# A two-layer hybrid SSM/retention/GLA backbone: opening chunks re-queued, modulation loads halved, norms rounded straight from PSUM, and layer 1's pack copies read from SBUF

## Chip, cores and metric

The kernel runs on one core of one Trainium2 chip. The metric is device time in microseconds for one execution; the time before is 1385.05 us, the median of three runs (1379.94, 1385.05, 1386.57).

## What is computed

Two layers of a diffusion backbone work on 256 latent tokens `x` and 256 context tokens `ctx`, D = 1024, all in fp32. Cut to what matters:

```
for l in range(2):
    m_l = split((silu(c)     @ w_mod[l] + b_mod[l]), 6)      # modulation vectors, latent
    m_c = split((silu(c_ctx) @ w_mod[l] + b_mod[l]), 6)      # modulation vectors, context
    p_l = split_in(modulate(rms_norm(x,   norm_mix[l]), m_l[0], m_l[1]) @ w_in[l])
    p_c = split_in(modulate(rms_norm(ctx, norm_mix[l]), m_c[0], m_c[1]) @ w_in[l])
    s5, ret, gla = three parallel token mixers on the columns of p_c, p_l
    x = x + m_l[2] * (merge(s5, ret, gla, gates) @ w_out[l])
    x = x + m_l[5] * swiglu(modulate(rms_norm(x, norm_ffn[l]), m_l[3], m_l[4]))
    # ctx gets the same two updates in layer 0 only
return rms_norm(x, norm_final)
```

`modulate(h, shift, scale)` is `h * (1 + scale) + shift`. Before anything of layer 0 can be projected, its first two modulation vectors (shift and scale, 2 x 1024 columns of `w_mod`, 8 MB) have to be computed.

## The kernel before

**Precision.** Every fp32 matmul is made of three matmuls in fp32r: an operand is split into a rounded part `hi` and a remainder `lo`, and `hi*hi + hi*lo + lo*hi` is summed. For weights, ACT writes `hi <- raw` (L228) and DVE writes `lo <- raw - hi` (L231); for activations the pair lives in `rb` (tile block, hi or lo, k, 128 tokens). Weights come through a ring of three `raw` buffers and four `hi`/`lo` pairs, loaded ahead of use by a scheduler's priorities.

**Who orders the work.** Code is traced with priorities, and a scheduler that simulates the engines decides the order in which each engine's instructions stand. At run time every engine takes its own list strictly from the front. `tc.issue_after(ins)` adds an order only: what is traced inside it on that engine stands behind `ins`. All loads named here (`in_w_mod`, `in_w_in`) are issued by SP in one list.

**The opening of layer 0** (`layer`, l == 0). The first D of the modulation is cut into four chunks c of 256 columns for shift and scale each. For each chunk: `mod_chunk` loads `w_mod` (two loads of 1 MB, one for each of m = 1 and 0), runs 8 + 64 small matmuls against `sil` (`b<-wm,one`, `b<-arena,sil` or `b<-zone,sil`), copies the result to SBUF on ACT (`arena<-b 128x128`), transposes it on PE and writes `mod` on DVE. `norm_chunk` transposes the chunk's 256 channels of all four token tiles into two PSUM banks (s = 0 context, 1 latent), modulates them on DVE (`arena<-b,mod`, multiply then add), rounds them on ACT (`rb<-arena`) and takes the remainder on DVE (`rb<-arena,rb`). `pack_weights` loads and splits the chunk's 512 KB of `w_in`, and `pack_mms` runs 24 matmuls of 128x128 by 128x512 into four banks that all four chunks add into. When chunk 3 is done, `pack_out` copies the four banks out (`arena<-b 128x512` on ACT, `perm` on DVE, L593), and `gla_v` starts: its weights are four loads of 416 KB, `raw 128x832`.

**Two places in layer 1.** `pack_early` and `pack` also end in `pack_out`, there with `lean=True`: ACT copies each bank to `res[x]`, and DVE reads the same bank again for the permuted copy `up` that is stored to DRAM. After the output projection, `out_tok` calls `norm_t` for tile 3 and then tile 2, and `ffn_in_tok` begins with `p == 0`: 24 matmuls for each tile. `norm_t` transposes a tile in two halves of four k; of each half ACT modulates two k and DVE two into `h32`, ACT rounds `h32` into `rb`, DVE takes the remainder.

Of the kernel before, what the change touches and what calls it, by code (L numbers as in the profile page):

```python
# [19 lines left out]
D = 1024  # L20
KD = 8
# [118 lines left out]
class Hybrid:  # L140
# [86 lines left out]
    def act(self, out, in_, f, scale=1.0, bias=0.0):  # L227
        self.S.activation(out, in_, f, bias=bias, scale=scale)  # L228
# [202 lines left out]
    def mod_chunk(self, c, brow):  # L431
# [3 lines left out]
        for m in (1, 0):  # L435
            ws[m] = (self.zone if c == 3 and m else self.arena).new(KD, 256)
            self.q["modc"].dma_start(out=ws[m].ap, in_=i["w_mod"][0][:, D * m + 256 * c:D * m + 256 * c + 256].rearrange(
                "(k p) c -> p k c", p=128))
# [12 lines left out]
        self.act(rows.ap, b[:, :128], AF.Copy)  # L451
        tb = self.bank()
# [8 lines left out]
    def norm_chunk(self, c, xs):  # L461
        ks = slice(2 * c, 2 * c + 2)
        h32 = self.new(4, 2, 128)
        for s in range(2):
            b = self.bank()
            for t in range(2):
                for k in range(2):
                    o = 128 * (2 * t + k)
                    self.transpose(b[:, o:o + 128], xs[2 * s + t].ap[:, 128 * (2 * c + k):128 * (2 * c + k) + 128])
            hv = h32.ap[:, 2 * s:2 * s + 2]  # L470
            bc = lambda a: a[:, None, ks, s:s + 1].to_broadcast([128, 2, 2, 128])
# [51 lines left out]
    def norm_t(self, l, which, t, x):  # L523
# [66 lines left out]
    def pack_out(self, pk, banks, u_dr, res=None, lean=False):  # L590
# [4 lines left out]
        for x in range(4):  # L595
# [3 lines left out]
            perm(up.ap[:, c0:], banks[x][:, c0:])  # L599
# [4 lines left out]
            if lean and x == 0:  # L604
                perm(up.ap[0:64, 0:256], banks[0][0:64, 0:256])
# [824 lines left out]
    def ffn_in_tok(self, l):  # L1430
# [3 lines left out]
        for p in range(KF // 2):  # L1434
# [10 lines left out]
            if not p:  # L1445
                self.tok_mms(banks, ws, (1, 0), range(KD), 0, KD - 1, h)
# [52 lines left out]
    def layer(self, l):  # L1499
# [5 lines left out]
        if l == 0:  # L1505
            with self.prio(-2 * W_AHEAD):
# [8 lines left out]
                banks = [self.bank(self.mm) for _ in range(4)]  # L1515
                for c in range(4):
# [3 lines left out]
                self.drop(*xs)  # L1520
            gqk = self.pack_out(0, banks, u_dr)
            self.load_params2()
# [8 lines left out]
        if l == 0:  # L1531
            self.s5d = [{}, {}]
            self.gd = [{m: self.dram.tile([2, D], F32, name=self.nm("gd")) for m in (2, 5)} for _ in range(2)]
            with self.inside(self.zone):
                self.s5_tables()
# [110 lines left out]
```

## Time and profile before

| | |
|---|---|
| Median of three runs | 1385.05 us |
| The profiled execution's own time | 1389.15 us |
| Its span, first to last instruction | 1387.1 us |
| PE busy | 1332.2 us, 96% of the span |
| DVE / ACT busy | 909.6 us (66%) / 579.1 us (42%) |
| Mean granted TensorE clock | 0.986 of 2.4 GHz |
| HBM read / written | 231.0 MB / 23.3 MB |

The profiled execution is 4.1 us longer than the median of the runs, and all sums below are made against it. In rows of the timeline the first number is the start in us, the second the length, then engine, line, operation, what it writes and reads, the count, and in brackets the idle time before it and what ended it. A clock of 1.00 is 2.4 GHz, 0.50 is 1.2 GHz.

### The profile page before, as it was taken

To read this page: it belongs to the slowest core of one execution; us is meant where nothing else is said; L and a number is where in the kernel's file an instruction comes from. 1 tells how busy PE (TensorE), PEld (TensorE's weight loads), DVE (VectorE), ACT (ScalarE), POOL (GpSimd) and SP (SyncE) were. 2 spreads that over 40 slices of the span, in tenths; PEclk is the share of its full clock that TensorE was granted. 3 is DMA by queue.
4 is the path that set the end of the run, shared out by engine and by line. 5 is a ranking of instruction groups with operands and counts; after the bars stand their busy time and mean duration, and the time that the engine had idled before them with its cause. 6 is when DMAs were issued, how large, how long until landed. Compare 5 with 4: busy or idle time off the path is not lost.

```text
span 1387.1 us, 20296 instructions
## 1 busy us (share of the span) xinstructions
PE 1332.2 (96%) x7723; PEld 1082.7 (78%) x7723; DVE 909.6 (66%) x1395; ACT 579.1 (42%) x920; POOL 73.7 (5%) x115
## 2 busy tenths in 40 slices
PE   4899999999999999999999999999999989899997
PEld 3788888777767778788777777898987867788886
DVE  4579682849879665535455687764696688655555
ACT  3367352333432233222222345544456544544453
POOL 3310000002000020000000000000000010000000
PEclk9999999999999999999999999999999989999999
DMA  9743455677877565633333787654655646465653
GB/s 308 205 123 106 153 167 165 228 220 236 280 245 216 200 184 170 215 92 106 119 115 116 250 310 245 197 158 122 181 160 189 199 145 213 149 194 187 213 183 106
DMA packets 202584, 255.63 MB, mean 184 GB/s; under 512 B 20704, under 2 KB 153100, under 8 KB 201976
## 3 DMA queue, kind: packets, MB, share of 16 engines
q1 hardware_dynamic: 189032, 228.05, 52.6%
q10 hardware_dynamic: 10240, 20.39, 4.1%
q0 software_dynamic: 3216, 5.91, 1.7%
q8 instruction: 61, 1.00, 0.3%
q14 instruction: 35, 0.29, 0.1%
HBM read 231.00 MB, written 23.30 MB: 183 GB/s over the span
## 4 chain that ended last, share of the span: by engine, by line
PE 81%; DMA 8%; DVE 5%; issue 2%; ACT 2%; SPq 1%; POOL 0%; DVEq 0%; ACTq 0%; POOLq 0%
PE b L243 79%; DMA wm<-in_w_mod_dram 4%; PE b L253 2%; DVE arena L231 1%; DVE zone L234 1%; DVE lo L231 1%; DMA arena<-in_w_mod_dram 1%; DMA raw<-in_w_in_dram 1%; ACT arena L228 1%; DMA arena<-udr 1%; ACT hi L228 1%; DMA arena<-sw 1%; DMA arena<-in_ctx_dram 0%; DMA raw<-in_w_ffn_out_dram 0%; DMA rb<-k 0%
## 5 line engine op out<-in xcount | busy, mean ns | idle before, releaser
L243 PE MATMUL b<-hi,rb 128*128 128x512 f32 (+2 forms) x1752 | 535.5, 383 | 5.5 <-DVE arena L593 3.5
L243 PE MATMUL b<-rb,hi 128*128 128x512 f32 (+1 forms) x1568 | 465.3, 378 | 1.4 <-DVE rb L231 1.4
L231 DVE TENSOR_TENSOR lo<-raw,hi 128x1024 fp32r<-128x1024 f32 (+3 forms) x295 | 333.7, 1136 | 201.4 <-ACT hi L228 198.5
L228 ACT ACTIVATE hi<-raw 128x1024 fp32r<-128x1024 f32 (+3 forms) x295 | 289.7, 989 | 419.4 <-PE b L243 275.0
L243 PEld LDWEIGHTS b<-hi,rb 128*128 128x128 f32 x1752 | 328.1, 189 | 67.4 <-issue 8.1
L243 PE MATMUL b<-lo,rb 128*128 128x512 f32 (+2 forms) x876 | 334.2, 382 | 0.9 <-DVE lo L231 0.9
L243 PEld LDWEIGHTS b<-rb,hi 128*128 128x128 f32 x1568 | 284.5, 189 | 64.5 <-issue 11.9
L243 PE MATMUL b<-rb,lo 128*128 128x512 f32 (+1 forms) x784 | 294.2, 376 | 0.0
L243 PEld LDWEIGHTS b<-lo,rb 128*128 128x128 f32 x876 | 166.2, 190 | 28.3 <-issue 1.6
L243 PEld LDWEIGHTS b<-rb,lo 128*128 128x128 f32 x784 | 147.9, 189 | 28.6 <-issue 3.4
L228 ACT ACTIVATE arena<-b 128x512 f32<-128x512 f32 (+7 forms) x168 | 79.1, 481 | 106.1 <-PE b L243 71.8
L243 PE MATMUL b<-arena 128*128 128x96 f32 (+9 forms) x1056 | 120.7, 289 | 0.8 <-ACT arena L228 0.8
L231 DVE TENSOR_TENSOR arena<-arena 128x512 f32<-128x512 f32 (+5 forms) x164 | 102.0, 640 | 17.2 <-ACT arena L228 14.9
L243 PEld LDWEIGHTS b<-arena 128*128 128x128 f32 (+6 forms) x1056 | 89.9, 160 | 24.3 <-issue 8.3
L234 DVE SCALAR_TENSOR_TENSOR arena<-arena,b 128x512 f32<-128x512 f32 (+1 forms) x124 | 72.3, 587 | 47.4 <-PE b L243 44.3
L234 DVE SCALAR_TENSOR_TENSOR zone<-wm,sil,zone 128x1024 f32<-128x1024 f32 x56 | 71.0, 1280 | 26.1 <-DMA wm<-in_w_mod_dram 26.0
L231 DVE TENSOR_TENSOR zone<-zone 128x512 f32<-128x512 f32 (+3 forms) x117 | 67.9, 604 | 28.5 <-DMA wb<-zone 17.4
L228 ACT ACTIVATE rb<-arena 128x256 fp32r<-128x256 f32 (+3 forms) x101 | 46.4, 476 | 61.5 <-PE b L243 33.6
L231 DVE TENSOR_TENSOR rb<-arena,rb 128x256 fp32r<-128x256 f32 (+2 forms) x106 | 53.7, 521 | 16.9 <-ACT rb L228 16.7
L253 PE MATMUL b<-cst,arena 128*128 128x128 f32 (+2 forms) x254 | 40.0, 284 | 19.4 <-DMA arena<-in_norm_mix_dram 8.9
L253 PEld LDWEIGHTS b<-cst,arena 128*128 128x128 f32 (+2 forms) x254 | 30.9, 146 | 27.3 <-issue 16.1
L228 ACT ACTIVATE arena<-arena 128x512 f32<-128x512 f32 (+3 forms) x62 | 36.7, 599 | 34.9 <-DVE arena L231 27.8
(145 smaller groups left out, 686.5 us busy)
## 6 DMA issues: line engine op xcount, KB each, us to landing
wm<-in_w_mod_dram SPq DMA_DIRECT2D x80, 512.0 KB
raw<-in_w_ffn_out_dram SPq DMA_DIRECT2D x66, 512.0 KB
raw<-in_w_in_dram SPq DMA_DIRECT2D x48, 512.0 KB
raw<-in_w_ffn_in_dram SPq DMA_DIRECT2D x44, 512.0 KB
raw<-in_w_ffn_in_dram SPq DMA_DIRECT2D x88, 256.0 KB
raw<-in_w_in_dram SPq DMA_DIRECT2D x48, 384.0 KB
raw<-in_w_out_dram SPq DMA_DIRECT2D x16, 512.0 KB
arena<-in_w_mod_dram SPq DMA_DIRECT2D x7, 1024.0 KB
```

Source lines behind the costliest of these rows:

```text
L228: self.S.activation(out, in_, f, bias=bias, scale=scale)
L231: self.last = self.V.tensor_tensor(out=out, in0=a, in1=b, op=op).ins
L234: self.last = self.V.scalar_tensor_tensor(out=out, in0=a, scalar=s, in1=b, op0=op0, op1=op1).ins
L243: self.last_mm = self.P.matmul(out, l, r, start=start, stop=stop, **k).ins
L253: self.last_tr = self.P.transpose(out, in_, self.ident[:k, :k]).ins
```

## The change

1. `mod_chunk` loads each chunk of `w_mod` as four loads of 512 KB, the first four k of both m ahead of the last four.
2. `norm_chunk` no longer goes through an SBUF copy to be rounded: for each k of each bank ACT writes the modulated and rounded value from PSUM into `rb`, DVE writes the unrounded one from the same PSUM columns into `h32`, and DVE takes the remainder per bank.
3. The opening's `pack_mms` of chunk c is traced behind the norm of chunk c + 1, and the ACT part of `pack_weights` stands behind the ACT copy of the chunk's modulation (`row_out`).
4. `load_params2` and `s5_tables` stand behind the opening's last matmul on PE, `s5_tables` also behind the last norm instruction on ACT.
5. `norm_t` is written as `norm_chunk` is now, four k on each engine.
6. With `lean`, `perm` reads ACT's SBUF copy, not the bank; ACT copies the context half of bank 0's first 64 partitions too.
7. `ffn_in_tok`, `p == 0`: for each tile first all `hi` by `hi` and `hi` by `lo` matmuls, then those with the tile's `lo`.

```diff
         for m in (1, 0):
             ws[m] = (self.zone if c == 3 and m else self.arena).new(KD, 256)
-            self.q["modc"].dma_start(out=ws[m].ap, in_=i["w_mod"][0][:, D * m + 256 * c:D * m + 256 * c + 256].rearrange(
-                "(k p) c -> p k c", p=128))
+        for kh in range(2):
+            for m in (1, 0):
+                self.q["modc"].dma_start(out=ws[m].ap[:, 4 * kh:4 * kh + 4], in_=i["w_mod"][0][
+                    512 * kh:512 * kh + 512, D * m + 256 * c:D * m + 256 * c + 256].rearrange("(k p) c -> p k c", p=128))
...
-            self.tt(hv, b.rearrange("p (t k c) -> p t k c", t=2, k=2), bc(self.mod[:, 0, 1]), ALU.mult)
-            self.tt(hv, hv, bc(self.mod[:, 0, 0]), ALU.add)
-        self.act(self.rb[:, 1:5, 0, ks], h32.ap, AF.Copy)
-        self.tt(self.rb[:, 1:5, 1, ks], h32.ap, self.rb[:, 1:5, 0, ks].bitcast(F32), ALU.subtract)
-        self.drop(h32)
+            for k in range(2):
+                kk = 2 * c + k
+                src = b[:, 256 * k:256 * k + 256].rearrange("p (t c) -> p t c", t=2)
+                self.act(self.rb[:, rows, 0, kk], src, AF.Identity, scale=sc[:, kk, s:s + 1], bias=sh[:, kk, s:s + 1])
+                self.ts(h32.ap[:, :, k], src, sc[:, kk, s:s + 1], sh[:, kk, s:s + 1], ALU.mult, ALU.add)
+            self.tt(self.rb[:, rows, 1, ks], h32.ap, self.rb[:, rows, 0, ks].bitcast(F32), ALU.subtract)
...
-                src, dst = b[:, 128 * k:128 * k + 128], h32.ap[:, kk]
-                if k < 2:
-                    self.act(dst, src, AF.Identity, scale=sc[:, kk, s:s + 1], bias=sh[:, kk, s:s + 1])
-                else:
-                    self.ts(dst, src, sc[:, kk, s:s + 1], sh[:, kk, s:s + 1], ALU.mult, ALU.add)
-            self.act(self.rb[:, 1 + t, 0, ks], h32.ap[:, ks], AF.Copy)
+                src = b[:, 128 * k:128 * k + 128]
+                self.act(self.rb[:, 1 + t, 0, kk], src, AF.Identity, scale=sc[:, kk, s:s + 1], bias=sh[:, kk, s:s + 1])
+                self.ts(h32.ap[:, kk], src, sc[:, kk, s:s + 1], sh[:, kk, s:s + 1], ALU.mult, ALU.add)
...
-            perm(up.ap[:, c0:], banks[x][:, c0:])
+            if lean and x == 0:
+                self.act(o.ap[0:64, 0:256], banks[0][0:64, 0:256], AF.Copy)
+            perm(up.ap[:, c0:], (o.ap if lean else banks[x])[:, c0:])
...
                 for c in range(4):
                     self.mod_chunk(c, brow)
                     self.norm_chunk(c, xs)
-                    self.pack_mms(banks, self.pack_weights(0, 0, c), c)
+                    with self.tc.issue_after(self.row_out):
+                        ws.append(self.pack_weights(0, 0, c))
+                    if c:
+                        self.pack_mms(banks, ws[c - 1], c - 1)
+                self.pack_mms(banks, ws[3], 3)
```

On ACT, where the opening's last two chunks stood before (`hi_501` is chunk 3's weights, `b_343` and `b_437` are the modulation of chunks 2 and 3, `hi_639` to `hi_726` are the first three weights of `gla_v`):

```order
L228 ACTIVATE hi_407<-raw_404 128x16x16
L228 ACTIVATE hi_501<-raw_498 128x16x48
L228 ACTIVATE hi_501<-raw_498 128x16x16
L228 ACTIVATE arena<-b_343 128x128
L228 ACTIVATE hi_639<-raw_636 128x832
L228 ACTIVATE hi_683<-raw_680 128x832
L228 ACTIVATE arena<-b_437 128x128
L228 ACTIVATE rb<-arena 128x4x256 x2
L228 ACTIVATE zone<-zone 128x32
L228 ACTIVATE hi_726<-raw_723 128x832
```

The same place on ACT in the changed kernel (`b_431` is chunk 3's modulation, `hi_501` its weights, `b_478` and `b_488` its two banks of transposed tokens, `hi_663` to `hi_750` the first three weights of `gla_v`):

```order
L228 ACTIVATE arena<-b_431 128x128
L228 ACTIVATE hi_501<-raw_498 128x16x48
L228 ACTIVATE hi_501<-raw_498 128x16x16
L228 ACTIVATE hi_663<-raw_660 128x832
L228 ACTIVATE hi_707<-raw_704 128x832
L228 ACTIVATE rb<-b_478,mod 128x2x128
L228 ACTIVATE rb<-b_488,mod 128x2x128
L228 ACTIVATE hi_750<-raw_747 128x832
L228 ACTIVATE rb<-b_478,mod 128x2x128
L228 ACTIVATE rb<-b_488,mod 128x2x128
```

The copy of a chunk's modulation now stands ahead of the weights, and one weight of `gla_v`, `hi_750`, stands between the first and second k of chunk 3's norm, where the before had its third weight behind the whole norm. DVE's list has the same shape: `lo_708` stands ahead of chunk 3's `mod`, and `lo_751` between the first and the second k. On SP the third weight's load, `raw_747`, now stands behind two loads of 512 KB of later modulation weights (`wm`); before, the third weight stood ahead of those two.

On PE, at the start of layer 1's FFN: before (`b_9656`, `b_9667` are tile 3's transposes, `b_9711`, `b_9722` tile 2's, `b_9734` and `b_9733` the sums of tiles 3 and 2):

```order
L253 MATMUL b_9656<-cst,arena 128x128 x4
L253 MATMUL b_9667<-cst,arena 128x128 x4
L253 MATMUL b_9711<-cst,arena 128x128 x4
L253 MATMUL b_9722<-cst,arena 128x128 x4
L243 MATMUL b_9734<-hi_9738,rb 128x512
L243 MATMUL b_9734<-lo_9739,rb 128x512
```

And in the changed kernel, with `b_9682`, `b_9696` for tile 3, `b_9743`, `b_9757` for tile 2, `b_9772`, `b_9771` the sums:

```order
L253 MATMUL b_9682<-cst,arena 128x128 x4
L253 MATMUL b_9696<-cst,arena 128x128 x4
L243 MATMUL b_9772<-hi_9776,rb 128x512
L243 MATMUL b_9772<-lo_9777,rb 128x512
L243 MATMUL b_9772<-hi_9776,rb 128x512
L243 MATMUL b_9772<-lo_9777,rb 128x512
L253 MATMUL b_9743<-cst,arena 128x128 x4
L243 MATMUL b_9772<-hi_9783,rb 128x512
L243 MATMUL b_9772<-lo_9784,rb 128x512
L243 MATMUL b_9771<-hi_9776,rb 128x512
```

Four FFN matmuls of tile 3 now stand between tile 3's and tile 2's transposes. Elsewhere the scheduler's lists differ in many small places; the largest on PE is in layer 0's gates, where the third of the groups `b<-zone,unit` that close a modulation vector summed on DVE stands 72 matmuls of 512 columns earlier than before.

## Rows read from the trace of the kernel before

**Rows 1.** The page: busy time, share of the span and instructions of each engine.
```profile
PE 1332.2 (96%) x7723; PEld 1082.7 (78%) x7723; DVE 909.6 (66%) x1395; ACT 579.1 (42%) x920; POOL 73.7 (5%) x115
```

**Rows 2.** Windows (us; busy PE, PEld, DVE, ACT, POOL; PEclk, DMA share, GB/s).
```profile
30.00:40.00 10.00, 9.98 (x78) 7.37 (x77) 4.09 (x7) 2.21 (x3) 6.07 (x12) 1.00 1.10 339
40.00:50.00 10.00, 7.53 (x102) 5.86 (x104) 5.07 (x12) 3.10 (x5) 3.47 (x7) 0.72 0.87 256
44.40:51.20 6.80, 6.30 (x81) 4.94 (x81) 6.03 (x12) 2.24 (x4) 2.57 (x6) 0.50 0.73 220
1187.90:1194.70 6.80, 4.69 (x15) 4.08 (x16) 6.16 (x12) 4.02 (x10) 0.56 (x1) 0.50 0.06 9
400.00:420.00 20.00, 17.00 (x84) 12.09 (x83) 16.50 (x20) 7.51 (x12) 0.00 (x0) 0.91 0.76 230
```

**Rows 3.** Timeline of SP's queue in the opening.
```profile
12.43 3.67 SPq L437 DMA_DIRECT2D arena<-in_w_mod_dram  x2
...
36.28 10.34 SPq L273 DMA_DIRECT2D raw<-in_w_in_dram  x6
47.69 0.82 SPq L357 DMA_DIRECT2D wm<-in_w_mod_dram  x2
```

**Rows 4.** Timeline of the opening's end, chunks 2 and 3.
```profile
41.35 1.07 PE L243 MATMUL b<-arena,sil 128*32 128x128 f32 x30
...
43.54 1.15 ACT L228 ACTIVATE hi<-raw 128x768 fp32r<-128x768 f32 x2 [7.21 <-DMA raw<-in_w_in_dram]
...
44.90 0.48 PE L253 MATMUL b<-cst,arena 128*128 128x128 f32 x1 [2.47 <-ACT arena L228]
...
46.51 0.90 ACT L228 ACTIVATE hi<-raw 128x832 fp32r<-128x832 f32 x1 [0.27 <-DMA raw<-in_w_in_dram]
...
47.73 1.02 DVE L231 TENSOR_TENSOR lo<-raw,hi 128x832 fp32r<-128x832 f32 x1
...
59.55 1.30 PE L243 MATMUL b<-rb,hi 128*128 128x512 f32 x5
...
65.00 0.35 PE L243 MATMUL b<-hi,rb 128*128 128x416 f32 x1
```

**Rows 5.** Timeline of chunk 0's norm: multiply, round, remainder.
```profile
22.20 1.29 DVE L231 TENSOR_TENSOR arena<-b,mod 128x512 f32<-128x512 f32 x2
...
24.72 1.06 ACT L228 ACTIVATE rb<-arena 128x1024 fp32r<-128x1024 f32 x1 [3.38 <-DVE arena L231]
...
25.81 1.23 DVE L231 TENSOR_TENSOR rb<-arena,rb 128x1024 fp32r<-128x1024 f32 x1 [1.12 <-ACT rb L228]
```

**Rows 6.** Timeline of layer 1's first norm, rounded from PSUM already.
```profile
915.64 2.84 ACT L228 ACTIVATE rb<-b,mod 128x256 fp32r<-128x256 f32 x6 [4.42 <-PE b L253]
916.24 2.37 DVE L240 TENSOR_SCALAR arena<-b,mod 128x256 f32<-128x256 f32 x5 [2.13 <-ACT rb L228]
...
919.57 0.68 DVE L231 TENSOR_TENSOR rb<-arena,rb 128x512 fp32r<-128x512 f32 x1
```

**Rows 7.** Timeline where layer 1's FFN begins.
```profile
1186.54 1.06 PE L253 MATMUL b<-cst,arena 128*128 128x128 f32 x8 [1.79 <-DVE arena L238]
...
1187.65 1.48 ACT L228 ACTIVATE arena<-b,mod 128x128 f32<-128x128 f32 x4
...
1190.01 1.94 PE L253 MATMUL b<-cst,arena 128*128 128x128 f32 x8 [2.41 <-DVE arena L238]
...
1191.61 0.78 PE L243 MATMUL b<-hi,rb 128*128 128x512 f32 x1
...
1192.61 1.05 PE L243 MATMUL b<-hi,rb 128*128 128x512 f32 x2
```

**Rows 8.** Timeline behind layer 1's second pack.
```profile
970.50 0.37 ACT L228 ACTIVATE arena<-b 128x256 f32<-128x256 f32 x1
...
971.18 0.74 DVE L593 COPY arena<-b 128x256 f32<-128x256 f32 x2
...
972.06 0.41 PE L243 MATMUL b<-hi,rb 128*128 128x384 f32 x1 [1.70 <-DVE arena L593]
```

More of the change, by code (lines that the diff above doesn't have):

```diff
@@ L227, in act @@
     def act(self, out, in_, f, scale=1.0, bias=0.0):
-        self.S.activation(out, in_, f, bias=bias, scale=scale)
+        self.last_act = self.S.activation(out, in_, f, bias=bias, scale=scale).ins
     def tt(self, out, a, b, op):
@@ L451, in mod_chunk @@
         self.act(rows.ap, b[:, :128], AF.Copy)
+        self.row_out = self.last_act
         tb = self.bank()
@@ L462, in norm_chunk @@
         ks = slice(2 * c, 2 * c + 2)
-        h32 = self.new(4, 2, 128)
+        sh, sc = self.mod[:, 0, 0], self.mod[:, 0, 1]
         for s in range(2):
             b = self.bank()
-            for t in range(2):
-                for k in range(2):
-                    o = 128 * (2 * t + k)
-                    self.transpose(b[:, o:o + 128], xs[2 * s + t].ap[:, 128 * (2 * c + k):128 * (2 * c + k) + 128])
-            hv = h32.ap[:, 2 * s:2 * s + 2]
-            bc = lambda a: a[:, None, ks, s:s + 1].to_broadcast([128, 2, 2, 128])
-            self.tt(hv, b.rearrange("p (t k c) -> p t k c", t=2, k=2), bc(self.mod[:, 0, 1]), ALU.mult)
-            self.tt(hv, hv, bc(self.mod[:, 0, 0]), ALU.add)
-        self.act(self.rb[:, 1:5, 0, ks], h32.ap, AF.Copy)
-        self.tt(self.rb[:, 1:5, 1, ks], h32.ap, self.rb[:, 1:5, 0, ks].bitcast(F32), ALU.subtract)
-        self.drop(h32)
+            h32 = self.new(2, 2, 128)
+            rows = slice(1 + 2 * s, 3 + 2 * s)
+            for k in range(2):
+                for t in range(2):
+                    o = 128 * (2 * k + t)
+                    self.transpose(b[:, o:o + 128], xs[2 * s + t].ap[:, 128 * (2 * c + k):128 * (2 * c + k) + 128])
+            for k in range(2):
+                kk = 2 * c + k
[3 more added lines that the diff above has]
+            self.tt(self.rb[:, rows, 1, ks], h32.ap, self.rb[:, rows, 0, ks].bitcast(F32), ALU.subtract)
+            self.drop(h32)
+        self.norm_act = self.last_act
     def gate_rows(self, gd):
@@ L604, in pack_out @@
             if lean and x == 0:
-                perm(up.ap[0:64, 0:256], banks[0][0:64, 0:256])
+                perm(up.ap[0:64, 0:256], o.ap[0:64, 0:256])
                 self.q["up"].dma_start(out=u_dr[128 * pk:128 * pk + 64, :, 0:32],
@@ L1445, in ffn_in_tok @@
             if not p:
-                self.tok_mms(banks, ws, (1, 0), range(KD), 0, KD - 1, h)
+                for t in (1, 0):
+                    for k in range(KD):
+                        for x in range(2):
+                            self.mm_(banks[t], h(t, k)[0], ws[k // 2][x][:, k % 2], k == 0 and x == 0, False)
+                    for k in range(KD):
+                        self.mm_(banks[t], h(t, k)[1], ws[k // 2][0][:, k % 2], False, k == KD - 1)
             gt = [self.new(256) for _ in range(2)]
@@ L1515, in layer @@
                 banks = [self.bank(self.mm) for _ in range(4)]
+                ws = []
                 for c in range(4):
@@ L1518, in layer @@
                     self.norm_chunk(c, xs)
-                    self.pack_mms(banks, self.pack_weights(0, 0, c), c)
+                    with self.tc.issue_after(self.row_out):
[3 more added lines that the diff above has]
+                self.pack_mms(banks, ws[3], 3)
                 self.drop(*xs)
+            pe, act = self.last_mm, self.norm_act
             gqk = self.pack_out(0, banks, u_dr)
-            self.load_params2()
+            with self.tc.issue_after(pe):
+                self.load_params2()
         else:
@@ L1533, in layer @@
             self.gd = [{m: self.dram.tile([2, D], F32, name=self.nm("gd")) for m in (2, 5)} for _ in range(2)]
-            with self.inside(self.zone):
+            with self.inside(self.zone), self.tc.issue_after(pe), self.tc.issue_after(act):
                 self.s5_tables()
```

## The prediction

> **What bounds the kernel now.** I read the page first: PE is busy 96% of the span, DVE 66% [rows 1]. A change can therefore win only where PE stands idle, runs at half clock, or has matmuls taken away, and none are taken away here. So I went through the waits of PE and the windows with a low granted clock, and then through the timeline of the three places where the change meets such a wait. The reader should see three things.
>
> First, the opening is bound by its loads: 339 GB/s from 30 to 40 us [rows 2], chunk 3's weights landed at 43.54, where ACT began to split them [rows 4]. That split stood in ACT's list ahead of chunk 2's modulation copy, although chunk 2's modulation matmuls had ended at 42.42; PE idled 2.47 us until 44.90 [rows 4], and from 44.4 to 51.2 its granted clock was 0.50, 1.2 GHz [rows 2]. Everything behind followed: pack of chunk 3 at 59.55, first `gla_v` matmul (`128x416`) at 65.00 [rows 4]. Second, at the start of layer 1's FFN two idle times of 1.79 and 2.41 us end at 1186.54 and 1190.01 [rows 7], and the clock is 1.2 GHz from 1187.9 to 1194.7 [rows 2]. Third, behind layer 1's second pack PE waits 1.70 us for DVE's copies [rows 8].
>
> PE has hardly a gap behind the opening, so I let what is saved there pass whole to the end. That is an assumption, and rival 2 takes it away.
>
> **Opening, term A.** Chunk 3's modulation weights stand ahead of 512 KB of its `w_in`, so they land about 512 KB / 339 GB/s = 1.5 us before 43.54, at 42.0. PE has then only the later half of their matmuls to do (the whole 72 take some 1.07/30 each): with the split loads the first half is done; 0.5 us more for the end gives 42.5. The 20 matmuls left of chunk 2's pack at (65.00 − 59.55)/24 = 0.227 us [rows 4] make 4.5 us: 47.0. Nine transposes (eight took 1.06 [rows 7]) end at 48.1, and the eight matmuls of the two packs left that need no remainder (1.8) at 49.9. From there PE needs the norm of chunk 3.
>
> That norm's `mod` stands behind `lo` of `gla_v`'s second weight on DVE: its `hi` began at 46.51 and took 0.90, the `lo` 1.02 [rows 4], so 48.4, and `mod` is there at about 48.8. Then the new queue decides. ACT has the third weight's `hi_750` between the first and second k. Its load stands on SP behind chunk 3's weights, two weights of 416 KB and two loads of 512 KB: with its own 416 KB that is 2272 KB after 43.54, 6.9 us at 339 GB/s or 9.1 us at the 256 GB/s of 40 to 50 us [rows 2], so 50.4 to 52.6; I take 51.5. Then `hi` 0.90, two Identities from PSUM at 2.84/6 = 0.47 each, the last multiply-add on DVE at 2.37/5 = 0.47 (both [rows 6]) give 53.8; DVE's own `lo_751` (1.02) lies beside the Identities. Two remainders of 0.68 [rows 6]: 55.2. Twenty matmuls of chunk 3 follow, 4.55 us: 59.7. PE will have been idle about 5 us before them, twice what came ahead of the half clock at 44.90, so part of them will run at 1.2 GHz. A stretch of 6.8 us at half clock [rows 2] loses 3.4 us; bounds are 0 and 3.4, and I take the middle, 1.7, since the eight matmuls before the wait and the 20 behind it are fewer than those of the old stretch. `gla_v` begins at 61.4 to 61.5: **A = 3.5 us**. Bounds: with the third weight at 52.6 and the whole 3.4 the start is 64.3, gain 0.7. If the weight is never late, the norm goes from 48.8 through five steps of 0.47 (ACT and DVE by turns on two banks) and two remainders to 52.5, the matmuls end at 57.1, gain 7.9.
>
> The new norm itself is no longer than the old one. Before, a bank took multiply and add (0.65 each), and a rounding of 1.06 and a remainder of 1.23 for both banks [rows 5]; from 22.20 to 27.04, 4.8 us. Now 5 × 0.47 + 1.36 = 3.7 us for both. By turns is how the row behaves: the first multiply-add at 916.24 waited for ACT's `rb` [rows 6].
>
> The Trainium skill, "PSUM — Partial Sum Buffer", section "PSUM bank collisions raise a hardware error", asks for just that: two engines must not touch one bank in the same partitions at once, reads against reads included. It speaks against the change, which gives ACT and DVE the same bank to read four times in turn; the trace agrees in its wait at 916.24. If the two could read side by side, the chain above would be two steps, about 0.9 us, shorter.
>
> **Layer 1's FFN, term B.** Four matmuls of tile 3 now stand ahead of tile 2's transposes. Before, PE idled 2.41 us there [rows 7]; they need only `hi` of tile 3's first k. At half clock two take 1.05, so four take some 2.0 us [rows 7], which fills the idle time before 1190.01 nearly whole if tile 3's first `rb` is there by 1188. ACT's four copies from 1187.65 took 1.48 [rows 7] and now write `rb` at once, so two of them are there at 1188.4: some 1.6 us of the 2.0 fall into idle time. I take **B = 1.5 us**. Bounds: 0 if tile 3's first k isn't earlier than before, 3.1 if the clock also returns earlier by half the 6.8 us stretch (1.6 to 1.7 us on top). The later place of the `lo` matmuls (`p == 0` rewritten) belongs to this: it only takes waits away.
>
> **Lean copies, term C.** PE began at 972.06, when DVE's second copy from the bank ended (971.18 + 0.74 = 971.92) [rows 8]. Now the banks come free with ACT: its last copy ended 970.50 + 0.37 = 970.87, and the new one for the first 64 partitions costs another 0.37: 971.24, **C = 0.7 us**. Bounds 0 (another wait right behind) and 0.9 (nothing added: the copy already lies beside PE's work).
>
> **Costed at nothing.** The parameter loads and tables of `load_params2` and `s5_tables` move behind the opening on engines that wait there anyway; if the tables were late, they would stop ACT long behind `gla_v`'s start, and PE has all of `gla_v` before it. The split modulation loads add eight issues on SP; the queue holds its loads ahead (six `raw` loads issued in a 10.34 us stretch [rows 3]), and the stream is full at 339 GB/s. Uncovered, two issues taking 0.82 us [rows 3], eight would cost 3.3 us; rival 4.
>
> A + B + C = 5.7 us: 1389.15 − 5.7 = 1383.45 against the profiled execution, which was 4.1 above the median; against the median 1385.05 − 5.7 = **1379.4 us**. What a measurement of this kernel can tell from no change is about 0.5%, 6.9 us: faster means below 1378.1, slower above 1392.0.
>
> **Rivals.**
> 1. *The third weight is never waited for.* The loads that stand ahead of it land at more than 339 GB/s or are issued earlier, since everything in the opening is earlier. A = 7.9, the sum 10.1, time 1375.0. For it: chunk 3's weights may land before 43.54, since the copies ahead of the splits free PE and the buffers sooner. Against it: 2272 KB from 43.54 to 50.0 would need 360 GB/s, more than the 339 of [rows 2], and the two weights of before (832 KB) came at 287 GB/s, ready at 46.51 [rows 4]. Chance 0.22.
> 2. *The saved time does not arrive.* PE's lists after the opening are all re-made, and a few waits of 2 us, as those of [rows 7], at new places eat it: net −2 to +2 around nothing to 3, time 1383 to 1387. Against it: 96% busy leaves few such places. Chance 0.13.
> 3. *Slower: the gates' modulation sums.* The third group `b<-zone,unit` stands 72 matmuls of 0.227 us, 16.3 us, earlier on PE, while it needs DVE's sums of weights that come through SP. Between 400 and 420 us DVE is busy 16.5 of 20 us and PE 17.0 [rows 2], so DVE has little room to be 16.3 us earlier. If it is not earlier at all, PE waits up to 16.3 us there: 1385.05 − 5.7 + 16.3 = 1395.7; with a third to a half of it 1385 to 1388. It decides once the added wait exceeds 5.7 us. Against it: the weights are loaded one or two places earlier in SP's list too. Chance 0.10, half of it slower by over 0.5%.
> 4. *The split loads cost their price.* Eight issues uncovered: 3.3 us off the gain, 1382.7. Chance 0.05. The Trainium skill, "DMA: Bandwidth & Descriptors", section "Anatomy of one DMA — SWDGE (gpsimd) path", gives each DMA of that path a fixed part of about 2 us besides its bytes; were it paid in series, by an estimate from that page eight more would cost 16 us. Those loads are SP's, on another path, and no run here shows this; the 339 GB/s of rows 2 speak against a serial price.
>
> **How the numbers follow.** The forecast case holds 0.50; 0.15 of it lies below 1378.1, where A or B comes out near their upper bounds. Faster: 0.15 + 0.22 = 0.37. Slower: half of rival 3 and 0.01 for the rest, 0.06. Same: 0.57. The range: 1389.15 and the median differ by 4.1 us and the three runs by 6.6, so cases are wide even with a right sum. All upper bounds (7.9 + 3.1 + 0.9 = 11.9) give 1373.1, and 2 us of the runs' spread below that 1371; all lower ones (0.7) 1384.3, rival 2 to 1387, and 1388 takes in the lighter half of rival 3. Range 1371 to 1388.
>
> **What would show it.** Right: the first `128x416` matmul at about 61.5; in front of it a wait of PE from about 50 to 55 ending with DVE's remainder, behind ACT's wait for `raw` between chunk 3's Identities; no half clock from 44.4 on but one from about 52. FFN matmuls before tile 2's transposes, and that idle time 1.5 us shorter. No DVE L593 ahead of the matmul behind the second pack. Wrong: no wait of ACT for the third weight (rival 1); new idle times of PE longer than 2 us between 66 and 1180 us (rival 2), above all ahead of `b<-zone,unit` (rival 3); chunk 3's weights later than 43.54 (rival 4).

## The result: 16 us slower

The changed kernel takes 1401.92 us, the median of 13 runs (1395.25 to 1407.03); the kernel before took 1385.92 us in 13 runs beside them (1379.94 to 1398.57). The ratio is 1.0114, 95% interval 1.0089 to 1.0139. The forecast was 1379.4 us, range 1371 to 1388: wrong in sign. The profiled execution took 1399.32 us, 10.2 us more than that of before; the two profiles show two thirds of the difference of the medians.

The page of the changed kernel, busy time as in [rows 1]:

```profile
PE 1348.2 (96%) x7723; PEld 1088.9 (78%) x7723; DVE 912.7 (65%) x1407; ACT 587.2 (42%) x940; POOL 77.2 (6%) x115
```

PE has the same 7723 matmuls and is busy 16.0 us longer; its idle time fell from 54.9 us (1387.1 − 1332.2) to 49.2. So the time did not go into more waiting in sum; between 66 and 1180 us, where the prediction looked for new idle times, it is 18.3 us for 18.8. The windows of the changed kernel (busy PE, PEld, DVE, ACT, POOL; granted clock, DMA share, GB/s), all of its stretches at 1.2 GHz but the kernel's last:

```profile
56.50:59.90 3.40, 3.40 (x10) 2.63 (x9) 0.69 (x1) 0.87 (x2) 0.00 (x0) 0.50 0.04 10
288.60:298.80 10.20, 10.20 (x32) 5.08 (x25) 6.34 (x12) 1.19 (x3) 0.00 (x0) 0.50 0.50 141
411.50:418.30 6.80, 5.44 (x13) 4.29 (x14) 6.80 (x11) 0.00 (x0) 0.00 (x0) 0.50 0.52 166
920.10:923.50 3.40, 3.40 (x18) 3.40 (x17) 2.74 (x5) 0.56 (x1) 0.00 (x0) 0.50 0.00 0
1008.80:1019.00 10.20, 9.72 (x37) 8.75 (x37) 8.22 (x17) 7.00 (x10) 0.00 (x0) 0.50 0.68 229
1121.50:1141.90 20.40, 15.27 (x99) 11.23 (x99) 17.43 (x34) 6.04 (x14) 3.46 (x2) 0.50 0.35 116
```

The same view of the kernel before, the stretches that [rows 2] does not show:

```profile
167.30:174.10 6.80, 6.80 (x32) 4.99 (x32) 2.84 (x4) 5.18 (x8) 0.00 (x0) 0.50 0.03 7
406.20:409.60 3.40, 3.07 (x13) 1.88 (x14) 2.16 (x3) 0.38 (x1) 0.00 (x0) 0.50 0.70 202
1119.60:1129.90 10.30, 6.39 (x48) 5.05 (x49) 8.86 (x18) 4.39 (x9) 1.68 (x1) 0.50 0.69 248
```

PE's busy time at half clock is 47.4 us after and, with the two stretches of [rows 2], 27.3 us before (the last stretch of each kernel left out): 20.1 us more, of which half, 10 us, is lost to the clock. That is book-keeping, not yet a cause. To see where the lag arises, I weighted each matmul with the median time of its form in the kernel before and compared at what time each kernel has done the same weight (us against the profile of before; minus is ahead):

```
at (us)   change   edits 1-4   edit 6   change, old order   only PE's order new
   80      -2.9      -1.9       -1.4         -4.7                -2.0
  160      -2.3      -1.1       -1.4         -3.1                -1.5
  520      +2.7      -5.7       -6.2         -8.3                -1.7
  960      +1.8      -4.3       -8.4         -9.8                +2.4
 1000      -0.6      -3.8      -10.8         -6.4                +4.7
 1020      +6.0      -3.3       -4.2         -7.2                +3.7
 1100      +6.5      -3.3       -3.8         -7.2                +6.5
 1120     +10.4      -3.3       +0.3         -7.2               +12.9
 1300     +10.4      -3.7       +1.2         -7.0               +10.6
```

The lists agree at 80, 520, 960 and 1300 us; inside a re-made stretch (160 and 1000 to 1120 us) a row hangs on the weights by up to 1 us. In the first column the opening leads by 2.9 us (3.5 were forecast), though the two columns with the old opening lead by 1.4 and 2.0 us too; layer 0 between 160 and 520 us turns that into a lag of 2.7, and layer 1 between 1000 and 1120 us adds 11. Nothing is edited in either stretch. The last four columns are experiments, told below. Single executions differ by some us in layer 0, also where nothing differs (−1.4 to −6.2 in the edit-6 column, whose layer 0 is that of before); the medians decide there.

The three edited places, in the timeline of the changed kernel. The opening's end:

```profile
50.11 1.02 ACT L228 ACTIVATE rb<-b,mod 128x256 fp32r<-128x256 f32 x2 [1.64 <-PE b L253]
50.71 1.00 DVE L240 TENSOR_SCALAR arena<-b,mod 128x256 f32<-128x256 f32 x2 [0.74 <-ACT rb L228]
...
51.53 0.90 ACT L228 ACTIVATE hi<-raw 128x832 fp32r<-128x832 f32 x1 [0.40 <-PE b L243]
52.33 1.00 ACT L228 ACTIVATE rb<-b,mod 128x256 fp32r<-128x256 f32 x2
52.46 1.02 DVE L231 TENSOR_TENSOR lo<-raw,hi 128x832 fp32r<-128x832 f32 x1 [0.75 <-ACT hi L228]
...
53.40 0.99 DVE L240 TENSOR_SCALAR arena<-b,mod 128x256 f32<-128x256 f32 x2
...
54.31 1.28 DVE L231 TENSOR_TENSOR rb<-arena,rb 128x512 fp32r<-128x512 f32 x2
55.65 0.50 PE L243 MATMUL b<-rb,hi 128*128 128x512 f32 x1 [3.26 <-DVE rb L231]
...
62.06 0.43 PE L243 MATMUL b<-hi,rb 128*128 128x416 f32 x1
```

Against [rows 4], `gla_v` begins at 62.06 instead of 65.00. The third weight stands between the two k of the norm on both engines, as the lists said. The copy of chunk 3's modulation, the first of this chain, waited for PE's matmuls until 44.90:

```profile
44.90 0.28 ACT L228 ACTIVATE arena<-b 128x128 f32<-128x128 f32 x1 [4.63 <-PE b L243]
```

The second pack of layer 1, to be read against [rows 8]:

```profile
971.49 0.58 ACT L228 ACTIVATE arena<-b 128x512 f32<-128x512 f32 x1
971.53 0.34 PE L243 MATMUL b<-hi,rb 128*128 128x384 f32 x1
...
972.95 0.74 DVE L596 COPY arena<-arena 128x256 f32<-128x256 f32 x2
```

PE's wait of 1.70 us is gone, and DVE's copies come behind PE's next matmuls. The start of layer 1's FFN, against [rows 7]:

```profile
1197.27 1.07 PE L253 MATMUL b<-cst,arena 128*128 128x128 f32 x8 [1.79 <-DVE arena L238]
...
1198.88 0.50 PE L243 MATMUL b<-hi,rb 128*128 128x512 f32 x1 [0.54 <-ACT rb L228]
1199.21 0.40 PE L243 MATMUL b<-lo,rb 128*128 128x512 f32 x1
1199.81 0.50 PE L243 MATMUL b<-hi,rb 128*128 128x512 f32 x1 [0.20 <-ACT rb L228]
...
1200.42 0.63 PE L253 MATMUL b<-cst,arena 128*128 128x128 f32 x4
```

FFN matmuls fill the wait of 2.41 us, but waits of 0.20 to 0.54 us come in its place.

And one place that no edit touches, layer 1's GLA and S5 steps in the changed kernel and then in the kernel before:

```profile
1004.83 0.34 PE L243 MATMUL b<-hi,rb 128*128 128x384 f32 x1
...
1007.28 2.31 PE L243 MATMUL b<-arena,zone 128*128 128x64 f32 x16 [2.10 <-DVE arena L231]
...
1117.23 6.96 PE L243 MATMUL b<-arena 48*128 48x128 f32 x50
...
1128.71 0.65 PE L243 MATMUL b<-rb,arena 128*32 128x128 f32 x8 [1.33 <-DVE arena L231]
...
1131.51 1.93 PE L243 MATMUL b<-rb,arena 128*32 128x128 f32 x32 [2.15 <-DVE arena L231]
```

```profile
1001.37 3.77 PE L243 MATMUL b<-arena,zone 128*128 128x64 f32 x32
...
1114.66 0.73 PE L243 MATMUL b<-hi,rb 128*128 128x512 f32 x2
...
1121.86 1.93 PE L243 MATMUL b<-rb,arena 128*32 128x128 f32 x32 [3.00 <-DVE arena L231]
```

Before, the S5 matmuls `b<-arena,zone` started without a wait, in one run of 32; now 16 of them stand where their input is 2.10 us from ready. Before, wide projections (`128x512`) stood as late as 1114.66, between the narrow matmuls of the GLA; now 50 narrow ones stand in one row, and no wide ones are left behind them to cover DVE, that is, to give PE something to do while DVE works.

One more wait is new, at layer 0's gates, in the changed kernel:

```profile
412.86 0.79 PE L243 MATMUL b<-rb,hi 128*128 128x512 f32 x1 [3.38 <-DVE rb L231]
```

### The profile page after: what moved, and what is told of

Same layout as the page of the kernel before. It is cut to its first block, busy times and chain, and to the rows that moved or that the text cites. A ratio compares the mean times of both kernels' runs of the same rounds, so it can differ in the third digit from the quotient of the medians.

```text
span 1397.4 us, 20314 instructions
## 1 busy us (share of the span) xinstructions
PE 1348.2 (96%) x7723; PEld 1088.9 (78%) x7723; DVE 912.7 (65%) x1407; ACT 587.2 (42%) x940; POOL 77.2 (6%) x115
## 4 chain that ended last, share of the span: by engine, by line
PE 81%; DMA 7%; DVE 6%; issue 3%; ACT 2%; SPq 2%; POOL 0%; ACTq 0%; DVEq 0%; POOLq 0%
PE b L243 79%; DMA wm<-in_w_mod_dram 3%; PE b L253 2%; DMA arena<-in_w_mod_dram 1%; DVE arena L231 1%; DVE zone L234 1%; DVE lo L231 1%; DMA raw<-in_w_in_dram 1%; SPq L439 1%; DMA arena<-in_x_dram 1%; ACT hi L228 1%; ACT arena L228 1%; DVE arena L240 1%; DMA arena<-sw 1%; ACT L228 0%
## 5 line engine op out<-in xcount | busy, mean ns | idle before, releaser
L243 PE MATMUL b<-rb,hi 128*128 128x512 f32 (+1 forms) x1568 | 472.1, 382 | 7.0 <-DVE rb L231 7.0
L243 PEld LDWEIGHTS b<-rb,hi 128*128 128x128 f32 x1568 | 288.2, 191 | 73.1 <-issue 12.4
L243 PE MATMUL b<-rb,lo 128*128 128x512 f32 (+1 forms) x784 | 297.2, 380 | 0.0
L228 ACT ACTIVATE arena<-b 128x256 f32<-128x256 f32 (+7 forms) x170 | 79.4, 480 | 110.5 <-PE b L243 82.3
L243 PE MATMUL b<-arena 128*128 128x96 f32 (+9 forms) x1056 | 124.4, 295 | 0.8 <-issue 0.7
L243 PEld LDWEIGHTS b<-arena 128*128 128x128 f32 (+6 forms) x1056 | 93.0, 164 | 25.7 <-issue 11.8
L231 DVE TENSOR_TENSOR rb<-arena,rb 128x256 fp32r<-128x256 f32 (+1 forms) x110 | 54.0, 506 | 15.9 <-ACT rb L228 15.6
L228 ACT ACTIVATE rb<-arena 128x256 fp32r<-128x256 f32 (+3 forms) x93 | 39.8, 446 | 57.7 <-PE b L243 45.0
L228 ACT ACTIVATE arena<-arena 128x512 f32<-128x512 f32 (+3 forms) x62 | 37.0, 601 | 29.7 <-DVE arena L231 20.1
L497 POOL TENSOR_TENSOR st<-st,mh 128x1 f32<-128x1 f32 x16 | 10.2, 637 | 671.8 <-DVE st L240 670.7
```

The source lines that it names most:

```text
L228: self.last_act = self.S.activation(out, in_, f, bias=bias, scale=scale).ins
L231: self.last = self.V.tensor_tensor(out=out, in0=a, in1=b, op=op).ins
L243: self.last_mm = self.P.matmul(out, l, r, start=start, stop=stop, **k).ins
L497: self.G.tensor_tensor(out=st[:, 3:4], in0=st[:, 2:3], in1=self.mh[:, 0:1], op=ALU.pow)
```

## The experiments

**Theory and rivals.** After the two profiles I held that the loss comes from the lists that the scheduler re-made behind the edits, and not from an edited instruction. Rivals: the edited instructions cost it themselves; or the opening's earlier start shifts everything behind it against its loads.

**Which edit loses where.** Four kernels with parts of the change, each part word for word from the diff above: edits 1 to 4 alone, edit 6 alone, edits 5 and 7 alone, and the change without edit 6. Edit 6, for instance, is its lines of that diff and one more copy, which that diff does not show:

```diff
-                perm(up.ap[0:64, 0:256], banks[0][0:64, 0:256])
+                perm(up.ap[0:64, 0:256], o.ap[0:64, 0:256])
```

In their lists the parts separate. By names and shapes, PE's list of the change differs from that of before at 2467 of 7723 places, far more than the "many small places" of the section on the change. Edits 1 to 4 re-make it in layer 0 up to the 2920th matmul (465 us in the kernel before) and leave layer 1's all but alone; edit 6 re-makes it from layer 1's first pack to its gates (659 places between 970 and 1128 us); edits 5 and 7 only where the FFN starts.

> Edits 1 to 4 alone, layer 1 as before. Theory (each re-made list costs where it was re-made): the trace of the change lags 2.7 us behind before from 520 us on, after a lead of 2.9 us at 80 us, so this kernel ends 2 to 4 us later than before, ratio 1.001 to 1.003, and its lag stays constant from 520 us to the end. Rival (layer 1's loss comes from the opening's shift, not from layer 1's own edits): about 10 us later, ratio 1.007, with the loss between 1000 and 1125 us.

> Edit 6 alone (the pack copies read from SBUF). Theory: 1.5 us won at the pack, then about 10.5 us lost between 1000 and 1125 us, so 8 to 10 us later than before, ratio 1.006 to 1.008, with half clock near 1009 and 1121 us. Rival (the loss belongs to the opening or to the FFN edit): 0 to 1.5 us earlier than before.

> Edits 5 and 7 alone (norm_t from PSUM, p == 0 rewritten). Theory: only the start of layer 1's FFN moves, 0.4 us earlier as the trace of the change shows, ratio 0.999 to 1.000. As predicted (term B): 1.5 us earlier.

> The change without edit 6. Theory: opening 2.9 us won, layer 0 loses 5.5, FFN wins 0.4, so 2 to 3 us later than before, ratio 1.001 to 1.003, some 8 to 10 us faster than the whole change. Rival (the losses are of the opening): ratio above 1.008, as the change itself.

Measured, against the kernel before (1387.82 us):

```
edits 1-4     1395.13 us   1.0062  [1.0034, 1.0090]
edit 6        1393.11 us   1.0054  [1.0032, 1.0077]
edits 5, 7    1386.32 us   1.0000  [0.9976, 1.0025]
without 6     1394.96 us   1.0060  [1.0031, 1.0088]
```

The parts add up: 0.62 + 0.54 + 0.00 = 1.16% for 1.14. Both places lose by themselves, and layer 1's loss does not need the opening, which puts the third rival away for layer 1. I had put the opening's part at 2 to 4 us from one profile; it is 7 to 9, so the change without edit 6, expected at 1.001 to 1.003, missed as well. The profiled execution of edits 1 to 4 was the fastest of its twelve (1385.15 us) and shows why one profile misled. Its PE list near 282 us is that of the change, with no fall of the clock there. The timeline of edits 1 to 4 alone, then of the change:

```profile
282.24 5.02 PE L243 MATMUL b<-arena 128*128 128x64 f32 x44
287.98 0.64 PE L243 MATMUL b<-wm,sil 128*32 128x256 f32 x8 [0.71 <-DMA wm<-in_w_mod_dram]
```

```profile
282.04 5.02 PE L243 MATMUL b<-arena 128*128 128x64 f32 x44
288.24 0.79 PE L243 MATMUL b<-wm,sil 128*32 128x256 f32 x8 [1.18 <-DMA wm<-in_w_mod_dram]
```

Half a microsecond more of waiting for `wm`, and the change ran the next 10.2 us at half clock where the other execution did not. Four traces have this PE list in layer 0, so that they can be compared row for row. In two of them the clock falls here: in the change after a wait of 1.18 us, 5.1 us lost against edits 1 to 4 alone, and in the change without edit 6 (1396.06 us, near its median), 6.5 us lost:

```profile
290.87 1.00 PE L243 MATMUL b<-wm,sil 128*32 128x256 f32 x8 [1.02 <-DMA wm<-in_w_mod_dram]
```

In the other two (0.71 us here, 0.95 in the filled kernel told below) it does not. In the 13 traces with the old list it never falls between 240 and 400 us; in the one of the kernel before, the `wm` matmuls that follow a narrow row there (292.75) do not wait. So in these traces layer 0's loss is mostly time at half clock, in a place that the new list made; that the longer wait makes the fall is not tested.

**Old work in the new order, new work in the old order.** A kernel can be held to another's lists by order edges between neighbours on each engine. They add no wait. The orders are tables of numbers taken from the other kernel; added instructions stand right behind their neighbour.

```diff
+def pin_order(k, tables, whole):
...
+        for n in order:
+            chain.append(seq[n])
...
+        for a, b in zip(chain, chain[1:]):
+            k.tc.add_manual_dep(b, a.name, mybir.DependencyInfo(
+                mybir.DependencyClass.NoSync, mybir.DependencyReason.DATA), reason="pin_order")
...
     k.final()
+    pin_order(k, TABLES, True)
```

> Edit 6 alone, but every engine's list is held to that of the kernel before (order edges only, no waits; the two added ACT copies stand right behind their neighbour). Theory (the re-made lists cost the time, not the edited instructions): the 1.5 us won at the pack remain, ratio 0.998 to 1.000. Rival (the edited copies themselves cost it, by what they read or by when the stores leave): as edit 6 alone, ratio 1.005.

> The kernel before, not one instruction edited, with every engine's list held to that of the kernel with edit 6 alone. Theory (lists): 8 to 10 us slower than before, ratio 1.005 to 1.007, half clock near 1009 and 1121 us. Rival (the edited copies): ratio 1.000.

> The whole change, with the lists between the opening's end and layer 1's output projection held to those of the kernel before. Theory (lists): the opening's 2.9 us, the pack's 1.5 and the FFN's 0.4 remain, 4 to 5 us faster than before, ratio 0.996 to 0.997. Rival (the edits' own work or a phase that they shift): as the change itself, ratio 1.011.

> Edits 1 to 4 alone, lists behind the opening held to those of the kernel before. Theory (lists): 2 to 3 us faster than before, ratio 0.998. Rival (the new opening itself costs, or its earlier start shifts the rest against its loads): as edits 1 to 4 alone, ratio 1.006.

Measured, against the kernel before (1385.39 us):

```
edit 6, old order          1389.62 us   1.0023  [0.9996, 1.0051]
before, edit 6's order     1401.43 us   1.0102  [1.0060, 1.0144]
change, old order          1384.09 us   0.9987  [0.9966, 1.0008]
edits 1-4, old order       1385.24 us   0.9982  [0.9958, 1.0006]
```

This decides it for the 16 us. The unedited kernel in edit 6's order loses 1.0%, 14 us by the ratio, without one edited instruction; the whole change in the old order loses nothing, where it lost 1.14% in its own, and so do edits 1 to 4. The rival that the edits themselves cost the 16 us is dead, and so is the opening's shift.

For edit 6 the size of its order's price is less clear. With the edited copies it is 1.0054 against 1.0023, 0.3%, and these intervals overlap. The 1.0% is the price with the old copies, which fit that order worse: PE waits 1.71, 2.15 and 1.37 us at the two packs, where edit 6 alone does not wait. And in the old order edit 6 has a price of its own. PE's list there is exactly that of before, so the traces compare row for row: 2.0 us are gained at the second pack, and 4.5 lost behind it, at a new wait for DVE with 3.4 us of half clock behind it. The timeline of edit 6 in the old order, then of the change in the old order:

```profile
981.99 1.08 PE L256 MATMUL b<-cst,arena 128*128 128x128 f32 x4 [3.58 <-DVE arena L234]
```

```profile
979.65 1.12 PE L256 MATMUL b<-cst,arena 128*128 128x128 f32 x4 [3.68 <-DVE arena L234]
```

Three expectations were off in size: the held change was to be 0.996 to 0.997 and its interval reaches from there to 1.0008; edit 6 in the old order was to be at most 1.000 and has an interval that reaches from 0.9996 to 1.0051; and the unedited kernel in the new order was to be 1.005 to 1.007. The opening's gain of 3 us that the traces show is not separable from no change in the medians, and no version here is shown to beat the kernel before.

**Which engine's list.** Again the unedited kernel; now one engine's list, or all but one, is held to the order of edit 6. The edit is the table alone:

```diff
 TABLES = {
     'PE': (
-        'c-jruQ^Vjo6h`5uZquYqn>6Xzwr$(CZR;D`wr$(CZQJ&o^Aq;Xe%B*OK$0azQYB5&B||bLOR^;>ITDhv<Vv1IBwq?7DlsXPxFn=V'
...
+        'c-jrugQDO%07cQJR+1)Zn{;g3wr$(Cb;q`C+qP}nwmt9t#5sFO5|Cs`kyJ^ObjgrR$&zfzkz5H%NWzjQ5s6An@})ouB`ygml441*'
...
```

> The kernel before unedited, PE's list held to that of edit 6 alone, all other engines' lists to those of before. If the place of the matmuls in PE's list costs the time (wide projections used up ahead of the narrow S5 and GLA steps): as with all lists new, ratio 1.005 to 1.010, half clock near 1009 and near 1115 to 1121 us. If the loads' order or DVE's order costs it: ratio 0.998 to 1.003.

> The kernel before unedited, SP's list of loads held to that of edit 6 alone, the other lists to those of before. If the loads' order costs the time: ratio 1.005 to 1.010 with PE waiting for weights near 1000 us. If PE's list costs it: ratio 0.998 to 1.002.

> The kernel before unedited, all lists held to those of edit 6 alone but SP's, which stays that of before. If PE's and DVE's lists cost the time: ratio 1.005 to 1.010. If the loads' order costs it: ratio 0.998 to 1.002.

Measured, against the kernel before (1385.90 us):

```
only PE's list new     1399.77 us   1.0088  [1.0065, 1.0111]
only SP's list new     1389.13 us   1.0018  [1.0000, 1.0035]
all new but SP's       1404.63 us   1.0126  [1.0097, 1.0154]
```

PE's list is enough for layer 1's loss. The loads' order costs 0.2% by itself, 0.35% at most by its interval, and it isn't needed for the loss; without it the loss is even above the 1.010 expected. No weights are needed between two rows that stand at the same place in all lists, 969 and 1135 us in the kernel before: there the five traces with edit 6's PE list lose 8.1 to 14.2 us, the ten others −0.9 to 6.4 (the 6.4 in the slowest execution of SP's list alone), and their stretch at half clock near 1120 us lasts 20.5 us in each of the five, 6.8 to 17.1 us in the others. The filled kernel below is left out of this. Of the two stretches at half clock that I expected only the second came. The timeline of the kernel with PE's list alone new:

```profile
1117.22 2.82 PE L246 MATMUL b<-arena 48*128 48x128 f32 x22
1120.25 3.83 PE L246 MATMUL b<-arena 128*128 128x96 f32 x18 [0.21 <-DVE arena L760]
1126.57 1.55 PE L246 MATMUL b<-arena 128*128 128x96 f32 x10 [2.49 <-DVE arena L760]
...
1136.27 1.11 PE L256 MATMUL b<-cst,arena 64*128 64x64 f32 x8 [1.66 <-ACT arena L231]
```

The changed kernel's wait of 2.10 us ahead of 1007.28 is not there (its S5 matmuls follow at once, 32 in one run), so that wait needs the other lists too; the row of narrow matmuls, and the waits for DVE behind them, need PE's order alone.

**Is it the clock?** The third test fills the narrow row. The change, held to its own lists, gets 32 matmuls of 128x256 into unused columns, whose results nobody reads:

```diff
+    def fill(self, out, n):
+        for _ in range(n):
+            self.mm_(out, self.rb[:, 4, 0, 0], self.rb[:, 4, 0, 1:1 + out.shape[1] // 128], True, True)
+            self.extra.append(self.last_mm)
...
                     self.mm_(pb[:, ts_], kt[d].ap[rs, ts_], qt[d].ap[rs, ts_], True, True)
+                    if l and p and t == t0:
+                        self.fill(pb[:, 256:512], 4)
```

and likewise behind the first token tile of `ob` and the first quarter of S5's read-out.

> The whole change with its own lists held, and 32 added matmuls of 128x256 whose results nobody reads, in eight groups of four: seven between the small matmuls of layer 1's last GLA and S5 steps, one in an earlier S5 step. They cost 32 x 0.12 = 4 us at full clock where PE would not wait anyway. Theory (the clock falls in the run of narrow matmuls near 1117 us, not by a wait): the fall at 1121 us comes later or not at all and the stretch of 20 us at half clock becomes 10 us or less, which pays for the fillers: ratio against before 1.007 to 1.012, lag gained between 1100 and 1125 us smaller than 4 us. Rival (the waits for DVE behind it make the fall, the narrow matmuls don't): half clock stays 20 us, and the time is 2 to 4 us above that of the change, ratio 1.013 to 1.015.

It took 1407.70 us, ratio 1.0168 [1.0137, 1.0198], some 6 us more than the change and above what either side expected. Its profiled execution was the fastest of its six (1399.81 us), so what follows is shown for one execution. Windows of the filled kernel, then of the change:

```profile
1113.80:1120.00 6.20, 6.20 (x43) 4.96 (x42) 2.67 (x5) 1.19 (x2) 0.00 (x0) 1.00 0.35 101
1120.00:1130.00 10.00, 6.13 (x64) 4.39 (x62) 8.34 (x14) 0.66 (x2) 0.00 (x0) 1.00 0.32 93
1130.00:1140.20 10.20, 7.18 (x51) 5.37 (x52) 7.47 (x15) 4.40 (x9) 1.68 (x1) 0.50 0.43 141
```

```profile
1114.00:1117.20 3.20, 3.20 (x29) 3.12 (x28) 2.12 (x6) 1.40 (x3) 0.00 (x0) 1.00 0.22 76
1117.20:1121.40 4.20, 4.11 (x37) 3.32 (x36) 3.36 (x7) 1.18 (x2) 0.00 (x0) 1.00 0.44 129
1121.40:1141.90 20.50, 15.37 (x100) 11.27 (x99) 17.54 (x34) 6.04 (x14) 3.46 (x2) 0.50 0.35 116
```

The theory was right on the clock in this execution and wrong on the time. With fillers the clock stays full through the narrow row and falls only at 1130, behind a wait: the stretch is halved, from 20.5 to 10.2 us. But nothing is won: the two PE lists are the same but for the fillers, and row for row the filled kernel falls 3.2 us behind the change between 1113 and 1143 us, as much as the 28 fillers there cost (28 x 0.12 = 3.4 us). The end of the place is not PE's. The timeline of the filled kernel:

```profile
1128.55 0.43 PE L246 MATMUL b<-rb,arena 128*32 128x128 f32 x8 [2.85 <-DVE arena L234]
1131.36 0.66 PE L246 MATMUL b<-rb,arena 128*32 128x128 f32 x8 [2.38 <-DVE arena L234]
```

A faster PE waits longer for DVE (2.85 and 2.38 us, where the change waited 1.33 and 2.15). DVE's scans and products between the S5 steps set the end there, and what PE's old order had were wide projections to do meanwhile. So I read the loss near 1120 us as lost cover, and the half clock as a mark of it. That more clock wins nothing is shown once; that wide projections put back there would win is read from the lists and not tested by itself.

**Parts of the opening.** Three kernels, one execution each, lists behind the opening held to the old order.

```diff
-        for kh in range(2):
-            for m in (1, 0):
-                self.q["modc"].dma_start(out=ws[m].ap[:, 4 * kh:4 * kh + 4], in_=i["w_mod"][0][
```

(the first, back to two loads a chunk; the second takes the old `norm_chunk`; the third has the split loads alone.)

> Edits 2 to 4 without the split loads, lists behind the opening held to those of before. If the split loads bring part of the opening's gain: gla_v starts 0.5 to 1.5 us later than in the held opening with all four edits (60.2 to 60.7 us). If they bring nothing: 60 to 61 us.

> Edits 1, 3 and 4 with the old norm through the SBUF copy, lists behind the opening held to those of before. If the norm from PSUM shortens chunk 3's chain by 1 us as the sum has it (3.7 for 4.8): gla_v starts near 61.5 us. If it brings nothing: 60 to 61 us.

> Edit 1 alone, lists behind the opening held to those of before. If eight more loads cost their issue time: gla_v starts 1 to 3 us later than in the kernel before (63.3 to 65.0 us). If they are covered: 63 to 65 us.

First `gla_v` matmul: 61.38 without the split, 61.12 with the old norm, 70.80 with the split alone. The first two are 0.4 to 1.2 us behind the two held openings with all four edits (60.18 and 60.73), in the direction expected, but within what the old opening differs by itself in eight traces (63.03 to 65.00). The third fell outside both expectations. Its stream is as full as before's (340 against 339 GB/s between 30 and 40 us), so no cost of the loads themselves shows. The timeline of ACT in it:

```profile
57.21 0.23 ACT L231 ACTIVATE zone<-zone 128x32 f32<-128x32 f32 x1 [7.65 <-DMA zone<-in_s_log_dt_dram]
57.38 0.90 ACT L231 ACTIVATE hi<-raw 128x832 fp32r<-128x832 f32 x1
58.18 0.26 ACT L231 ACTIVATE arena<-b 128x128 f32<-128x128 f32 x1
```

In this list the first instruction of `s5_tables` stands ahead of chunk 3's modulation copy, and ACT waits 7.65 us for a small parameter load. That is the order which edit 4 forbids; in the kernel before it stood behind the norm, where it cost nothing. Again an order, made by an edit that doesn't speak of it.

## Why the prediction was wrong, step by step

- **The step that failed** is the sentence "I let what is saved there pass whole to the end", and with it rival 2, which sized the re-made lists at "net −2 to +2". Rival 2 named the cause, re-made lists, and had its price and its way wrong. Edits 1 to 4 lose 0.80% by their new lists (1.0062 against 0.9982), the whole change 1.3% (1.0114 against 0.9987), edit 6 between 0.3 and 1.0%. Its sign came, with waits of 3.38 us at 412.86, 2.10 at 1007.28 and 2.15 at 1131.51; but waits of before went in their place (2.23 at 405.33, 1.70 at 972.06, 3.00 at 1121.86), and PE's idle time between 66 and 1180 us is no longer than before. What grew is PE's busy time, by 16.0 us, 10 of them at half clock.
- **Rival 3** gave the sign of the time, but not its place or its reason. PE does not wait for `b<-zone,unit` any more (2.8 us before). The 3.38 us near there are for `rb`, whose remainder on DVE stands behind a sum of `wm`; the two nearly cancel, and 16.3 us were feared.
- **"96% busy leaves few such places"** was the wrong inference. A list can open new places that the profile of before cannot show. In layer 1 the spare time was not in gaps; by my reading it was cover that PE's order gave to DVE's chains, and a list that spends wide matmuls early takes it away. In layer 0 the new place is the narrow row near 288 us with a wait for `wm` behind it.
- **Term A** came near by luck. The forecast ended chunk 3's modulation matmuls at 42.5, half of them done ahead, and then had ACT wait for the third weight until 51.5. They ran together and ended at 44.8, `mod` stood at 49.97 for 48.8, and ACT began that weight's `hi` at 51.53 because the norm itself was late: it did not wait for `raw`. PE waited 3.26 us for some 5. What held: the remainders end at 55.59 for 55.2, and a stretch of 3.4 us at half clock follows, 1.7 us lost as taken. In the one profile 2.9 us are won for 3.5. But eight traces of the old opening begin `gla_v` at 63.03 to 65.00 (median 63.7) and four of the new one in its own order at 62.06 to 63.79 (median 63.2): some 0.5 us.
- **The third weight's queue** was real, but not by its load. Its price was its own 0.90 on ACT and 1.02 on DVE in the middle of the norm. In the held order, where it stands behind the norm, the remainders end at 53.8 and 54.4 and `gla_v` begins at 60.18 and 60.73. Rival 1 (57.1) left out that the 20 matmuls also meet a half clock.
- **By turns on a bank**: ACT's pair starts at 50.11 and DVE's only 0.60 later, after a wait of 0.74 for ACT's `rb`. The Trainium skill, "PSUM — Partial Sum Buffer", section "PSUM bank collisions raise a hardware error", asks for such turns; the trace agrees. It cost nothing that the sum had not counted.
- **Term B** was 1.5 us and is 0.4 by the lag, 0.00% [−0.24, +0.25] in the runs. The four matmuls did move into the wait, but behind them ACT's `rb` and DVE's remainders are no earlier, and PE waits for these in pieces.
- **Term C** was 0.7: the whole wait of 1.70 us is gone, also where PE's list is that of before (2.0 us gained there, row for row), so its bound of 0.9 was too low. But its other bound, "another wait right behind", came too in the old order: 3.58 us, some 19 us on.
- **Split loads at nothing** held as to the stream (336 GB/s from 30 to 40 us after, 339 before), so rival 4 didn't come.

Left open: why one PE list loses the clock in some executions and not in others (edits 1 to 4 ran from 1385.15 to 1403.09 us, with mean granted clocks of 0.990 and 0.980); which engine's list costs layer 0 its part, which was only held as a whole (the PE list is re-made there, but it was not tried alone); and how much of edit 6's loss is its order's when its copies are the edited ones.

## What to carry to other kernels

Where a scheduler writes the lists, an edit has two prices: that of its instructions, and that of every list it re-makes behind itself; compare the lists first, and count a re-made stretch as a cost of unknown sign with a size of its own, here up to 1%. Where two kernels have the same list on PE, compare their traces row for row: it shows where time is lost without any weights. Before judging an edit, hold the rest to the old order (or the old work to the new one): it takes one run each way and tells the edit from its side effects. A busy share of 96% says nothing about how much cover an order gives: look at which wide matmuls stand beside the other engines' chains.

## What the hardware showed unexpectedly

- The clock fell to 1.2 GHz while PE was not idle: busy 3.20 of 3.20 and 4.11 of 4.20 us just ahead of the fall at 1121.4, all of it narrow matmuls (128x96, 128x64, then 48 rows by 48x128). In the one trace with 24 matmuls of 128x256 strewn between the same ones (of the other eight, four stand earlier and four behind the later fall) it did not fall there but at 1130.0.
- DVE's permuted fp32 copy of 128x512 is hardly faster from SBUF than from PSUM: 667 against 685 ns on average over the change's packs; of 128x256 it is no faster, 442 ns against 410 in the kernel before.
